# First bytes of the tiles of a decoder trunk, and the order of its mixer's steps

## The chip, the cores and the metric

The kernel runs on one core of one Trainium2 chip. The metric is the device time of one execution in microseconds; the time before is the median of three runs. The profile is that of one execution, taken by the hardware profiler. All times inside it count from the start of its span.

## The reference, cut to what matters

The input is one sequence of 512 tokens with 1024 channels, in float32. There are two layers; each is a mixer and then an MLP, and both of these parts are normed before (`rms_norm`) and after, and added to the residual stream.

```python
def trunk(x):
    for layer in (0, 1):
        h = rms_norm(x, mix_pre_g[layer])
        if layer == 0:                      # averages over 2, 4, 8, 16 tokens, less the token itself,
            m = pool_mixer(h, pool_w, pool_scale)   # then a 256x256 map for each of 4 channel groups
        else:                               # stick-breaking attention, 16 heads of 64; its k and v
            q = h @ w_q                     # were made from x after layer 0
            m = stick_breaking_attention(q, k, v) @ w_o
        x = x + rms_norm(m, mix_post_g[layer])
        h = rms_norm(x, mlp_pre_g[layer])
        u = h @ w_up[layer]                 # 1024 -> 4096
        x = x + rms_norm(square(relu(u)) @ w_down[layer], mlp_post_g[layer])   # 4096 -> 1024
        if layer == 0:
            k, v = split(rms_norm(x, kv_norm_g) @ w_kv)
    return x
```

## The kernel before, in words

**Three products for one.** Nearly all matrix products are made of a high and a low part of each operand, both in a 4-byte type that TensorE takes in one pass (fp32r). `split` makes them: ScalarE casts the high part, VectorE subtracts it from the source for the low part. A product is then three matmuls: high by high, high by low, low by high. Each matmul loads its 128x128 stationary operand (a LDWEIGHTS, PEld in the profile) and streams a moving operand of up to 512 columns (2048 bytes of each partition) past it. The load for the next matmul runs while the one before it streams.

**The stages.** The mixer of layer 0 comes first (some 49 us). Its work is cut into about 180 small steps, and `MIX_ORDER` lists them by hand: the letter is a step, the digits are a tile of 128 tokens and a half of the channels (tile 4 is the border between tiles, the tile `edge`). Every engine executes its own steps in this order. `q` squares a row of x on ScalarE and sums it, `r` takes the power of the sum on GpSimd, `b` scales the band matrix on VectorE, `P` averages on TensorE, `c` copies the result into `yt` on ScalarE, `L` scales the 256x256 maps on VectorE, `M` multiplies by them on TensorE, `s` and `g` square and weight what comes out, `T` transposes the normed tile, `H` and `X` split the transpose into `xnh` and `xnl`, and `U` is the first half (256 tokens) of one of the first four up products of the MLP.

Then come the MLP of layer 0 (to 366 us), its norms, the attention (to about 636 us) and the MLP of layer 1 (to the end).

**The MLP.** The up product of one block of 128 hidden channels (`up_block`) is 8x3 matmuls: a block of the weight is stationary (tiles `w` and `wx`, two halves high and low), the transposed tokens `xnh` and `xnl` move.

```python
for k in range(KC):     # L606 to L609; wh and wl are the two halves of a tile w
    nc.tensor.matmul(pu[:, cols], wh[:, k, :], xnh[:, k, cols], start=k == 0, stop=False)
    nc.tensor.matmul(pu[:, cols], wh[:, k, :], xnl[:, k, cols], start=False, stop=False)
    nc.tensor.matmul(pu[:, cols], wl[:, k, :], xnh[:, k, cols], start=False, stop=k == KC - 1)
```

Of the 32 blocks of hidden channels 28 go down through Strassen's seven products (class `Seven`, in five groups of two or three pairs of blocks), and the last four through a plain product (`contract`, lines L267 to L269, tiles `sq` and `dn`). In a Strassen product the tokens' operand `a` is stationary (made in `left`) and the weights' operand `w` moves (made in `right`). Both have two buffers, which take turns. A product is 12 matmuls in the first group and 18 in the others (L497); between two products one or two up blocks of the next group run.

**The attention.** The k and q projections are also `up_block`s (one pair of heads each), the v projection is a `contract`-like loop with 256 columns, and the output projection is `contract` again, with `ohl` (the heads' outputs) stationary and `w` moving; for the last two of its eight channel blocks the weights lie in the attention's own tiles `v`, `h` and `l`.

**First bytes.** The tiles are laid out one behind another in each partition, in the order in which they are first asked for, so that the size of a small tile sets the first byte of all that come behind it. The small tiles `gc` (96 bytes) and `stat` (32 bytes each) lie ahead of the large ones. In the program as built the first bytes are, for the tiles that TensorE reads most:

| tile | read as | before | modulo 256 | after | modulo 256 | after, modulo 512 |
|---|---|---|---|---|---|---|
| `xnh`, `xnl` | moving (up), stationary (v) | 17536, 33920 | 128, 128 | 17664, 34048 | 0, 0 | 256, 256 |
| `w`, `wx` | stationary (up), moving (output) | 96000 and every 8192 | 0 | 96256 and every 8192 | 0 | 0 |
| `a` of the products | stationary | 168704, 174848 | 0, 0 | 168960, 175360 | 0, 0 | 0, 256 |
| `w` of the products | moving | 187136, 199424 | 0, 0 | 187904, 201216 | 0, 0 | 0, 0 |
| `ohl` | stationary | 208192 and every 4096 | 64 | 208640 and every 4096 | 0 | 256 |
| `v`, `h`, `l` of the attention | moving (output), stationary | 145728, 170304, 175424 | 64 | 146176, 170752, 175872 | 0 | 256 |
| `sq`, `dn` | stationary, moving | all | 0 | all | 0 | 0 |

The pieces of a tile that a single matmul reads begin whole multiples of 512 bytes behind its first byte.

Of the kernel before, what the change touches and what calls it, by code (L numbers as in the profile page):

```python
# [42 lines left out]
    (w[0], [int(c) for c in w[1:]])  # L43
    for w in """z8 S0 q0 C0 S1 r0 b0 z1 P00 L00 L02 C1 c00 P01 L03 q4 L01 L13 r4 L10 L11 c01 L12 M00 M01 b4 q1 r1 b1 s00
    q2 s01 g00 e0 r2 P40 c40 g01 E0 b2 A0 P10 q3 c10 P11 r3 w0 P20 b3 v0 c11 M10 N00 P30 N01 h0 M11 T00 P31
    l0 s10 h1 c30 g10 s11 l1 c20 e1 g11 H00 E1 A1 X00 c31 h2 T01 M30 M31 w1 v1 l2 s30 N10 s31 M20 H01 N11 T10
    g31 P21 X01 H10 T11 c21 H11 M21 s21 X10 X11 e3 s20 g30 E3 U0 A3 w3 g21 e2 g20 h3 E2 A2 w2 v3 U1 N30 N31
    v2 l3 N21 T30 H30 U2 T21 T31 H31 N20 H21 T20 X30 X31 H20 X21 X20 U3""".split()
]
# [11 lines left out]

EDGE, REST, BORDER = 30, 114, 46

R_SCALE, R_MIX_POST0, R_MLP_PRE0, R_MLP_POST0, R_MIX_POST1, R_MLP_PRE1, R_MLP_POST1 = range(7)
# [5 lines left out]
def trunk(ctx, tc, x, consts, gcol, grow, pw, wup, wdn, wq, wk, wv, wo, out):  # L70
# [12 lines left out]
    def name(s):  # L83
        uid[0] += 1
        return f"{s}{uid[0]}"
# [6 lines left out]
    ident = keep.tile([P, P], F32, tag="ident", name="ident")  # L92
    gc = keep.tile([P, 3 * KC], F32, tag="gc", name="gc")
    for n in NS:
# [310 lines left out]
    class Seven:  # L405
# [17 lines left out]

        def __init__(self, l, first, n, mp):
            self.l, self.first, self.n, self.mp = l, first, n, mp
            self.banks, self.written, self.operands = {}, None, {}

        def load(self, second):
# [15 lines left out]
        def left(self, i):  # L444

            n, key = self.n, self.PRODUCTS[i][1]
            lo, hi = slice(0, S // 2), slice(S // 2, S)
            r11, r21, r12, r22 = (self.r[:, k, :n, h] for k in range(2) for h in (lo, hi))
            if i == 0:
                self.s1 = self.mp.tile([P, MOST, S // 2], F32, tag="s1", name=name("s1"))  # L450
            s1 = self.s1[:, :n]
            sub = lambda out, x, y, op=ALU.subtract: nc.gpsimd.tensor_tensor(out=out, in0=x, in1=y, op=op)  # L452
            if key == "s3":
                sub(s1, r21, r22, ALU.add)
                sub(r21, r11, r21)
                sub(r11, s1, r11)
            elif key == "r22":
                sub(r11, r12, r11)
            src = {"r11": r11, "s3": r21, "s2": r11, "r22": r22, "s1": s1, "r12": r12, "s4": r11}[key]
            a = self.mp.tile([P, 2, MOST, S // 2], F32R, tag="a", bufs=2, name=name("a"))  # L460
            split(src, a[:, 0, :n], a[:, 1, :n])
            return a

        def right(self, i):
# [15 lines left out]
            src = {"w11": w11, "t3": e, "t2": e, "t4": e, "t1": w12, "w21": w21, "w22": w22}[key]  # L480
            w = self.mp.tile([P, 2, MOST, 512], F32R, tag="w", bufs=2, name=name("w"))
            split(src, w[:, 0, :n], w[:, 1, :n])
# [25 lines left out]
    def mlp(l, mp, update):  # L508
# [4 lines left out]
        plain = 2 * sum(GROUPS)  # L513
        groups = [Seven(l, firsts[g], n, mp) for g, n in enumerate(GROUPS)]

# [96 lines left out]
    with tc.tile_pool(name="mix0", bufs=1, reuse_waits="tile") as mp:  # L612
# [9 lines left out]
        for w in windows.values():  # L622
            nc.vector.memset(w[:, D:], (EPS * D) ** 0.5)

# [59 lines left out]
        def squares(t):  # L684
            sts[t] = keep.tile([P, 8], F32, tag=f"stat{t}", bufs=4, name=name("stat"))
            mean_square(t, 0)
# [126 lines left out]
    with tc.tile_pool(name="att", bufs=1, reuse_waits="tile") as ap:  # L813
# [260 lines left out]
```

## Time and profile before

| | |
|---|---|
| time, median of 3 runs | 972.52 us (972.29 to 977.75) |
| the profiled execution: its time, its span | 971.85 us, 970.0 us |
| mean granted TensorE clock | 0.997 |
| TensorE busy | 951.6 us, 4761 matmuls |
| VectorE, ScalarE, GpSimd busy | 709.8, 568.7, 144.2 us |
| DMA | 157 MB, 45% of the 16 engines' span |

A row of the groups names the line, the engine, the operation, the tiles (out<-in), the shapes and the count; behind the first bar stand the busy time of the group and the mean nanoseconds of one. Matmuls overlap: one of 512 columns is busy for some 390 ns, but the next one starts some 230 ns after it. So what a matmul costs is the distance between two starts, and that is read from the starts in the timeline, or from the lengths in the chain of work that ended last, where a row "x18" is as long as it took until the next row began.

### The profile page before, as it was taken

The page shows a single profiled execution, that of the slowest core. Times are in us where ns is not written, and L with a number is a line of the kernel's source. Part 1 is how long each engine was busy: PE and PEld are TensorE (multiplying, and loading weights), DVE is VectorE, ACT ScalarE, POOL GpSimd, SP SyncE. Part 2 cuts the span into 40 slices and gives each one's busy share as a digit, 9 for nine tenths or more (in the row PEclk, how much of TensorE's full clock was granted, in tenths as well). Part 3 has the DMA queues.
Part 4 walks back from the last instruction along what each step waited for, and adds up shares of the span by engine and source line. Part 5 has one row for each costly group of instructions (what it writes and reads, how often), then busy time and mean ns, then how long its engine had stood idle before and what let it go on. Part 6 is the DMA issues. An engine that isn't in the chain of part 4 may idle for free.

```text
span 970.0 us, 12402 instructions
## 1 busy us (share of the span) xinstructions
PE 951.6 (98%) x4761; PEld 801.0 (83%) x4761; DVE 709.8 (73%) x736; ACT 568.7 (59%) x974; POOL 144.2 (15%) x108
## 2 busy tenths in 40 slices
PE   8999999999999999999999999989999999999997
PEld 6998888888888889888788887888888888888885
DVE  4856797988969966576477787855596876857856
ACT  6657889788865636455655563555544444443632
POOL 2120310502204014000000000301130300403103
PEclk9999999999999999999999999999999999999999
DMA  7544879697696840521624243332503233132012
GB/s 260 187 140 147 309 265 372 228 330 278 232 333 262 304 151 2 217 88 44 244 104 174 88 153 109 131 111 85 191 26 134 105 123 117 44 130 109 29 37 87
DMA packets 43683, 157.03 MB, mean 162 GB/s; under 512 B 4494, under 2 KB 4878, under 8 KB 43625
## 3 DMA queue, kind: packets, MB, share of 16 engines
q1 hardware_dynamic: 43625, 156.25, 45.0%
q8 instruction: 37, 0.61, 0.2%
q14 instruction: 21, 0.17, 0.1%
HBM read 122.68 MB, written 33.55 MB: 161 GB/s over the span
## 4 chain that ended last, share of the span: by engine, by line
PE 92%; DVE 3%; ACT 2%; issue 1%; DMA 1%; SPq 0%; POOL 0%; DVEq 0%; POOLq 0%; ACTq 0%
PE ps L497 28%; PE ps L609 15%; PE ps L607 15%; PE ps L608 15%; PE ps L268 4%; PE ps L269 4%; PE ps L267 4%; PE ps L957 2%; PE ps L947 1%; PE ps L731 1%; DVE e L929 1%; PE ps L915 1%; PE ps L916 1%; DMA edge<-in_x 1%; PE ps L708 1%
## 5 line engine op out<-in xcount | busy, mean ns | idle before, releaser
L497 PE MATMUL ps<-w,a 128*128 128x512 f32 x1176 | 278.8, 390 | 0.0
L608 PE MATMUL ps<-xnl,w 128*128 128x512 f32 (+1 forms) x712 | 265.0, 372 | 0.1
L609 PE MATMUL ps<-xnh,w 128*128 128x512 f32 (+1 forms) x712 | 265.1, 373 | 0.0
L607 PE MATMUL ps<-xnh,w 128*128 128x512 f32 (+1 forms) x712 | 265.0, 373 | 0.0
L497 PEld LDWEIGHTS ps<-w,a 128*128 128x128 f32 x1176 | 220.9, 188 | 47.4
L608 PEld LDWEIGHTS ps<-xnl,w 128*128 128x128 f32 x712 | 134.3, 189 | 25.2 <-DVE xnl L247 0.3
L609 PEld LDWEIGHTS ps<-xnh,w 128*128 128x128 f32 x712 | 134.1, 188 | 25.4
L607 PEld LDWEIGHTS ps<-xnh,w 128*128 128x128 f32 x712 | 134.0, 189 | 24.4
L134 DVE TENSOR_TENSOR w<-raw,w 128x1024 fp32r<-128x1024 f32 x62 | 82.2, 1328 | 62.7 <-ACT w L132 62.7
L132 ACT CAST w<-raw 128x1024 fp32r<-128x1024 f32 x62 | 65.0, 1049 | 87.8 <-PE ps L609 83.4
L506 DVE TENSOR_TENSOR y<-ps,y 128x512 f32<-128x512 f32 x124 | 83.4, 684 | 39.7 <-PE ps L497 39.7
L246 ACT CAST a<-r 128x768 fp32r<-128x768 f32 (+1 forms) x60 | 47.5, 792 | 70.5 <-PE ps L497 46.8
L452 POOL TENSOR_TENSOR s<-r 128x768 f32<-128x768 f32 (+1 forms) x10 | 20.5, 2048 | 382.0 <-ACT r L530 382.0
L247 DVE TENSOR_TENSOR a<-r,a 128x768 fp32r<-128x768 f32 (+1 forms) x60 | 60.1, 1004 | 18.5 <-ACT a L246 18.4
L246 ACT CAST w<-e 128x1536 fp32r<-128x1536 f32 (+1 forms) x30 | 42.0, 1398 | 44.5 <-DVE e L471 33.2
L292 POOL TENSOR_TENSOR y<-y,grow 128x512 f32<-128x512 f32 x12 | 18.7, 1556 | 316.4 <-ACT xn L250 316.4
L452 POOL TENSOR_TENSOR r<-r 128x768 f32<-128x768 f32 (+1 forms) x20 | 52.2, 2608 | 59.3 <-DVE a L247 58.5
L247 DVE TENSOR_TENSOR w<-e,w 128x1536 fp32r<-128x1536 f32 (+1 forms) x30 | 55.9, 1862 | 3.1 <-ACT w L246 2.7
L929 DVE TENSOR_TENSOR_SCAN e<-u,begin 128x1280 f32<-128x1280 f32 x16 | 45.1, 2822 | 13.3 <-ACT u L923 13.0
L143 ACT ACTIVATE apart<-apart,gc 128x128 f32<-128x128 f32 (+1 forms) x132 | 43.0, 405 | 0.0
L250 ACT ACTIVATE xn<-y 128x512 f32<-128x512 f32 (+1 forms) x25 | 15.4, 615 | 41.8 <-DVE y L359 41.8
L247 DVE TENSOR_TENSOR w<-xn,w 128x1536 fp32r<-128x1536 f32 (+1 forms) x20 | 33.0, 1651 | 6.4 <-ACT w L246 6.4
(137 smaller groups left out, 1486.5 us busy)
## 6 DMA issues: line engine op xcount, KB each, us to landing
raw<-in_wup SPq DMA_DIRECT2D x62, 512.0 KB, 4.1
w<-kept SPq DMA_DIRECT2D x58, 512.0 KB, 4.1
kept<-wx SPq DMA_DIRECT2D x30, 512.0 KB, 4.3
w<-in_wdn SPq DMA_DIRECT2D x8, 1536.0 KB, 6.7
kept<-apart SPq DMA_DIRECT2D x24, 512.0 KB, 3.6
xn<-in_wdn SPq DMA_DIRECT2D x8, 1536.0 KB, 8.0
raw<-in_wdn SPq DMA_DIRECT2D x8, 512.0 KB, 3.7
apart<-in_wk SPq DMA_DIRECT2D x7, 512.0 KB, 6.5
```

What stands on the lines that cost most here:

```text
L132: nc.scalar.copy(hi, raw)
L134: nc.vector.tensor_tensor(out=lo, in0=raw, in1=hi.bitcast(F32), op=ALU.subtract)
L143: nc.scalar.mul(c, c, gc[:, lo + k : lo + k + 1])
L246: latest["act"] = nc.scalar.copy(hi, src)
L247: latest["dve"] = nc.vector.tensor_tensor(out=lo, in0=src, in1=hi.bitcast(F32), op=ALU.subtract)
L452: sub = lambda out, x, y, op=ALU.subtract: nc.gpsimd.tensor_tensor(out=out, in0=x, in1=y, op=op)
L497: nc.tensor.matmul(bank, a[:, x, q, TS[t]], w[:, z, q], start=start and q == 0 and k == 0, stop=q == self.n - 1 and k == 2, skip_group_che ...
L506: nc.vector.tensor_tensor(out=part, in0=bank, in1=part, op=ALU.add)
L607: nc.tensor.matmul(pu[:, cols], wh[:, k, :], xnh[:, k, cols], start=k == 0, stop=False)
L608: nc.tensor.matmul(pu[:, cols], wh[:, k, :], xnl[:, k, cols], start=False, stop=False)
L609: nc.tensor.matmul(pu[:, cols], wl[:, k, :], xnh[:, k, cols], start=False, stop=k == KC - 1)
L929: nc.vector.tensor_tensor_scan(out=e[:, ::-1], data0=u[:, 1:][:, ::-1], data1=begin[:, ::-1], initial=0.0, op0=ALU.mult, op1=ALU.max,)
```

## The change

Three things, none of which changes what is computed. Small tiles are padded (`gc` by 128 bytes, the `stat` of the border by 32 in each of its four buffers, `u1` by 220), which moves the first bytes of the tiles behind them as in the table. The tiles `a` and `w` of the Strassen products become flat with 256 and 1024 spare bytes, and in layer 1 (only there: `self.l`) product number 7g+i, of the 35, puts its `a` at byte 64 times (7g+i) modulo 5 of the tile, and its `w` at entry (7g+i) modulo 7 of 0, 64, 128, 192, 256, 512 and 1024 bytes, so that each of the 35 pairs comes once. And `MIX_ORDER` is another list of the same steps.

```diff
+A_PLACES, W_PLACES = (0, 16, 32, 48, 64), (0, 16, 32, 48, 64, 128, 256)
...
-    gc = keep.tile([P, 3 * KC], F32, tag="gc", name="gc")
+    gc = keep.tile([P, 3 * KC + 32], F32, tag="gc", name="gc")[:, : 3 * KC]
...
+        def place(self, i, places):
+            return places[(7 * self.g + i) % len(places)] if self.l else 0
...
-            a = self.mp.tile([P, 2, MOST, S // 2], F32R, tag="a", bufs=2, name=name("a"))
+            a = self.mp.tile([P, MOST * S + 64], F32R, tag="a", bufs=2, name=name("a"))
+            at = self.place(i, A_PLACES)
+            a = a[:, at : at + MOST * S].rearrange("p (x n c) -> p x n c", x=2, n=MOST)
...
-            w = self.mp.tile([P, 2, MOST, 512], F32R, tag="w", bufs=2, name=name("w"))
+            w = self.mp.tile([P, MOST * D + 256], F32R, tag="w", bufs=2, name=name("w"))
+            at = self.place(i, W_PLACES)
+            w = w[:, at : at + MOST * D].rearrange("p (x n c) -> p x n c", x=2, n=MOST)
...
-            sts[t] = keep.tile([P, 8], F32, tag=f"stat{t}", bufs=4, name=name("stat"))
+            sts[t] = keep.tile([P, 16 if t == T else 8], F32, tag=f"stat{t}", bufs=4, name=name("stat"))
...
-        us = [ap.tile([P, NSEG + 1], F32, tag=f"u{a}", name=f"u{a}") for a in range(2)]
+        us = [ap.tile([P, NSEG + 1 + 55 * a], F32, tag=f"u{a}", name=f"u{a}")[:, : NSEG + 1] for a in range(2)]
...
-    for w in """z8 S0 q0 C0 S1 r0 b0 z1 P00 L00 L02 C1 c00 P01 L03 q4 L01 L13 r4 L10 L11 c01 L12 M00 M01 b4 q1 r1 b1 s00
+    for w in """z8 q0 S0 r0 C0 b0 S1 z1 P00 L01 C1 L02 L00 P01 L03 L12 c00 c01 M00 q4 L10 r4 L11 s00 L13 b4 q1 r1 M01 s01
```

What the new list does to the engines shows at two places. The first is ScalarE at the start of the mixer: `junk,stat<-edge` is step `q4`, `yt<-ps` are the copies `c00` and `c01`, `junk,stat<-ps` are the squares of a mixed tile. Before:

```order
L723 COPY yt<-ps_143 128x4x128
L679 ACTIVATE junk,stat_158<-edge 90x1025
L723 COPY yt<-ps_152 128x4x128
L679 ACTIVATE junk,stat_179<-x_71 128x1025
L250 ACTIVATE junk,stat_134<-ps_167 128x512
```

And now:

```order
L731 COPY yt<-ps_143 128x4x128
L731 COPY yt<-ps_152 128x4x128
L687 ACTIVATE junk,stat_166<-edge 90x1025
L251 ACTIVATE junk,stat_132<-ps_161 128x512
L687 ACTIVATE junk,stat_175<-x_71 128x1025
```

The second copy stood behind the step that reads `edge`; now it stands ahead of it. The second place is VectorE behind the scaling of the maps: `band<-bands` are the steps `b` (90 partitions is `b4`), `stat<-stat` is step `e0`, which adds two sums of squares. Before:

```order
L667 SCALAR_TENSOR_TENSOR pw_100<-pw_100,gc,scale 128x256 x4
L698 TENSOR_SCALAR band_177<-bands,stat_158 90x184
L698 TENSOR_SCALAR band_182<-bands,stat_179 128x456
L739 TENSOR_TENSOR m_188<-ps_167,grow_112 128x512
L743 TENSOR_SCALAR stat_134<-stat_134 128x1
```

And now:

```order
L675 SCALAR_TENSOR_TENSOR pw_100<-pw_100,gc,scale 128x256 x4
L706 TENSOR_SCALAR band_173<-bands,stat_166 90x184
L751 TENSOR_SCALAR stat_132<-stat_132 128x1
L706 TENSOR_SCALAR band_194<-bands,stat_175 128x456
L747 TENSOR_TENSOR m_216<-ps_161,grow_112 128x512
```

The sum `e0` now stands ahead of `b1`, the band for the first whole tile. Behind the mixer the order of instructions is the same on every engine, but for a few neighbours that change places.

More of the change, by code (lines that the diff above doesn't have):

```diff
@@ L43 @@
     (w[0], [int(c) for c in w[1:]])
-    for w in """z8 S0 q0 C0 S1 r0 b0 z1 P00 L00 L02 C1 c00 P01 L03 q4 L01 L13 r4 L10 L11 c01 L12 M00 M01 b4 q1 r1 b1 s00
[L45 to L48, printed above, removed]
+    for w in """z8 q0 S0 r0 C0 b0 S1 z1 P00 L01 C1 L02 L00 P01 L03 L12 c00 c01 M00 q4 L10 r4 L11 s00 L13 b4 q1 r1 M01 s01
+    e0 P40 b1 P11 P10 q2 c40 r2 c11 E0 q3 g00 b2 g01 r3 c10 P21 A0 b3 M11 w0 M10 s11 c21 v0 P31 N00 g11 s10
+    T00 P30 h0 M21 e1 c31 g10 E1 c30 N01 A1 P20 H00 T01 w1 X00 h1 v1 l0 s21 N11 M30 T11 c20 N10 T10 H01 M20
+    l1 H11 X11 H10 X10 s30 M31 X01 h2 s20 h3 g21 l2 s31 g20 e2 g30 E2 e3 E3 U0 A2 w2 g31 U1 A3 v2 U2 l3 N20
+    w3 T20 H20 v3 N31 T31 N30 N21 T30 H31 X20 X31 T21 H30 X30 U3 H21 X21""".split()
 ]
@@ L422, in trunk, with __init__ @@
         )
-        def __init__(self, l, first, n, mp):
-            self.l, self.first, self.n, self.mp = l, first, n, mp
+        def __init__(self, l, g, first, n, mp):
+            self.l, self.g, self.first, self.n, self.mp = l, g, first, n, mp
             self.banks, self.written, self.operands = {}, None, {}
+        def place(self, i, places):
+            return places[(7 * self.g + i) % len(places)] if self.l else 0
         def load(self, second):
@@ L513, in mlp @@
         plain = 2 * sum(GROUPS)
-        groups = [Seven(l, firsts[g], n, mp) for g, n in enumerate(GROUPS)]
+        groups = [Seven(l, g, firsts[g], n, mp) for g, n in enumerate(GROUPS)]
         steps = [n for n in range(1, 34)] if l == 0 else []
@@ L622, in trunk @@
         for w in windows.values():
-            nc.vector.memset(w[:, D:], (EPS * D) ** 0.5)
+            nc.vector.memset(w[:, D : D + 2], (EPS * D) ** 0.5)
         BANDS = (P, REST, BORDER)
```

## The prediction

> **What bounds the kernel now.** I read the totals and the chain of work that ended last first, then the busy times of the three long stages.
>
> ```profile
> PE 951.6 (98%) x4761; PEld 801.0 (83%) x4761; DVE 709.8 (73%) x736; ACT 568.7 (59%) x974; POOL 144.2 (15%) x108
> PE 92%; DVE 3%; ACT 2%; issue 1%; DMA 1%; SPq 0%; POOL 0%; DVEq 0%; POOLq 0%; ACTq 0%
> 49.00:366.00 317.00, 317.00 (x1425) 260.71 (x1424) 258.45 (x232) 231.64 (x384) 57.58 (x26) 1.00 0.71 256
> 385.00:636.00 251.00, 244.35 (x1436) 215.06 (x1435) 175.71 (x210) 136.15 (x302) 10.57 (x12) 0.99 0.37 133
> 636.00:955.00 319.00, 319.00 (x1443) 262.94 (x1443) 223.16 (x201) 152.91 (x187) 52.66 (x24) 1.00 0.27 94
> ```
>
> TensorE bounds it: 92% of the chain, and in the two MLPs (first and third stretch) it is busy for the whole stretch, at the full granted clock (1.00). So what changes the distance between two matmuls there changes the time one for one, while the next engine, VectorE with 258.45 of 317 us, has room.
>
> The second look is at that distance. The groups, with shapes kept apart, show that matmuls of one shape are not equal:
>
> ```profile
> L497 PE MATMUL ps<-w,a 128*128 128x512 f32 x1176 | 278.8, 390 | 0.0
> L607 PE MATMUL ps<-xnh,w 128*128 128x512 f32 x568 | 224.4, 395 | 0.0
> L267 PE MATMUL ps<-dn,sq 128*128 128x512 f32 x60 | 23.5, 392 | 0.0
> L268 PE MATMUL ps<-w,ohl 128*128 128x512 f32 x56 | 22.4, 399 | 2.2 <-DVE w L134 2.2
> ```
>
> All stream 512 columns. The Strassen products (L497) and the plain down product (`dn`, `sq`) last 390 to 392 ns, the up products (L607, and L608 and L609 with it) and the output projection (`ohl`) 395 and more. The chain of the second MLP and the timeline of one up block give the distances:
>
> ```profile
> 742.10 4.10 PE ps L497 x18
> 761.48 8.18 PE ps L497 x36
> ...
> 798.55 0.39 PE L607 MATMUL ps<-xnh,w 128*128 128x512 f32 x1
> ...
> 804.14 2.22 PE L497 MATMUL ps<-w,a 128*128 128x512 f32 x9
> ```
>
> One product is 18 matmuls in 4.10 us, two in a row 8.18, so the second takes 4.08: 226.7 ns each. (The 0.02 us that the first takes more are the turn from the up block before it.) The up block's 24 matmuls take from 798.55 to 804.14, 5.59 us: 232.9 each. The difference is 6.2 ns.
>
> What differs is the first bytes. I call the distance of a pair the first byte of the moving operand less that of the stationary operand which is loaded meanwhile, modulo 256. From the table of first bytes: products 0, `dn` with `sq` 0, up products 128 (`xnh` at 128, `w` at 0), output projection 192 (`w` at 0, `ohl` at 64). The longer ones are those whose distance is not 0. That it is the distance, and not whether each operand begins at a multiple of 256, shows where the output projection takes its weights from `h` and `l`, which begin at 64 as `ohl` does, and then again from `w`:
>
> ```profile
> 601.40 0.39 PE L269 MATMUL ps<-h,ohl 128*128 128x512 f32 x1
> ...
> 602.30 0.39 PE L267 MATMUL ps<-w,ohl 128*128 128x512 f32 x1
> ...
> 603.71 0.39 PE L267 MATMUL ps<-w,ohl 128*128 128x512 f32 x1
> ```
>
> The last four of the run with `h` and `l` take 0.90 us, 225 ns each; the next six, with `w`, 1.41 us, 235 each. Same line, same stationary tile, nothing waited for.
>
> At 256 columns there is no such difference:
>
> ```profile
> 36.07 0.28 PE L608 MATMUL ps<-xnl,w 128*128 128x256 f32 x1
> ...
> 41.23 0.29 PE L609 MATMUL ps<-xnh,w 128*128 128x256 f32 x1
> ...
> 959.95 0.28 PE L268 MATMUL ps<-dn,sq 128*128 128x256 f32 x1
> ...
> 962.59 0.28 PE L269 MATMUL ps<-dn,sq 128*128 128x256 f32 x1
> ```
>
> 43 steps in 5.16 us at distance 128, 22 steps in 2.64 us at distance 0: 120 ns both. Half up blocks and the v projection, all of 256 columns, so count nothing.
>
> **The change part by part.** *Padding, up products of the MLPs.* `xnh`, `xnl` and `w` all go to multiples of 256: distance 0. Each MLP has 28 whole up blocks (the first four are cut in halves), 672 matmuls, 1344 in both, all on a full TensorE: 1344 x 6.2 ns = **-8.3 us**. One thing in it is unknown: modulo 512 the new distance is 256, which no pair of this trace has (all the short ones are 0 modulo 512, and tiles that differ by 512 were among them). Its cost is bounded by the two rows above, 226.7 and 232.9, or may lie outside them. I take 226.7: the same products had 0 and 512 alike, so the period is 512 or a part of it; 64 and 128 are excluded as periods, since 192 and 128 are long; and the sizes speak for the smaller one. By the rows at both widths, 256 more columns cost 226.7 - 120.0 = 106.7 ns, so the 512 columns alone are 213.4 and the rest 13.3 ns; of a long pair the rest is 19.5. That is two units of some 6.6 ns against three. A load takes 512 bytes of each partition, which is two turns of a period of 256: two meetings, and three where they don't begin in step. With a period of 512 it would be one against one and a half. This is a fit, not a proof: I hold 256 the likelier, about three to one.
>
> *Padding, attention.* 1704 up matmuls (3 x 568) less 1344 are 360 in the k and q projections; of the output projection 148 go from distance 192 to 0 (modulo 512 to 256). 508 x 6.2 = 3.2 us. Here the chain is not TensorE's throughout:
>
> ```profile
> 447.73 0.60 ACT u L923
> 466.67 0.50 PE ps L267
> 568.83 0.62 ACT ah L246 x2
> 583.56 0.50 PE ps L268
> 614.55 0.72 ACT xn L250 x2
> 634.00 1.94 PE ps L324 x8
> ```
>
> Between the first and second, third and fourth, fifth and sixth of these rows it runs over ScalarE and VectorE: 19 + 15 + 19 = 53 of 251 us, in which a faster TensorE only waits longer. I count the other 79%: **-2.5 us** (bounds 0 and -3.2).
>
> *Products of layer 0.* Distance 0 stays 0 modulo 256. The turns of 0.02 us from an up block to a product go, some 30 of them: **-0.5 us**. Modulo 512 the two buffers of `a` now differ, so that every second product has 256: the same unknown.
>
> *Products of layer 1.* From the 35 pairs, 11 have distance 0 modulo 256, and of the 588 matmuls 422 have another: at 6.2 ns **+2.6 us**. A distance of 64 (146 matmuls) is not in the trace; bounds -0.9 and, at twice the price, +0.9 against that; I take the price of 128 and 192, which agree.
>
> *The mixer's list.* The rows of its start:
>
> ```profile
> 4.75 7.44 DMA edge<-in_x
> 12.37 1.06 ACT L679 ACTIVATE junk<-edge 90x1025 f32<-90x1025 f32 x1 [3.56 <-DMA edge<-in_x]
> 13.42 0.56 ACT L723 COPY yt<-ps 128x512 f32<-128x512 f32 x1
> 13.89 1.06 ACT L679 ACTIVATE junk<-x 128x1025 f32<-128x1025 f32 x1
> 15.07 0.60 ACT L250 ACTIVATE junk<-ps 128x512 f32<-128x512 f32 x1
> 14.18 0.31 DVE L698 TENSOR_SCALAR band<-bands,stat 90x184 f32<-90x184 f32 x1 [2.24 <-POOL stat L690]
> 14.04 1.99 PE L731 MATMUL ps<-pw,yt 128*128 128x256 f32 x8 [2.62 <-ACT yt L723]
> 15.87 1.88 PE L708 MATMUL ps<-band,edge 90*128 90x46 f32 x16
> 17.57 2.91 PE L708 MATMUL ps<-band,x 128*128 128x114 f32 x24
> 35.41 0.47 PE L607 MATMUL ps<-xnh,w 128*128 128x256 f32 x1
> ```
>
> `c01` (13.42) stood behind `q4`, which waited for the DMA of `edge`; M01 on TensorE waited 2.62 us for it, and P40 (15.87) for M01. Ahead of `q4` the copy is done by 9, and M01 well before 14. P40 then waits for its band alone (14.18 + 0.31), and begins at 14.55: 1.3 us sooner. Next, P11 needs `b1`, which now stands behind `e0`, and that waits for ScalarE's `s01`: q4 to 13.5, s00 0.7, q1 1.2, s01 0.7, so 16.1, and `b1` is done by 16.7. P40 takes 1.70 and ends at 16.25: 0.45 us of the gain is lost. From there to the end of U3 TensorE has the same matmuls as before and was busy without a gap worth naming, so if no other step is late the stage ends **-0.9 us** sooner. What is late next would be VectorE's chain from `A2` over `A3` to `N20`, ahead of the transposes that stand between U2 and U3; they have the 8.6 us of U0 to U2 to hide under. Bounds -1.3 (no wait at all) and +1 (a wait of 2 us there).
>
> Nothing else moves. **Sum:** -8.3 - 2.5 - 0.5 + 2.6 - 0.9 = -9.6. Against the profiled execution's own 971.85 us (span 970.0) that is 962.3; the median of the three runs is 0.7 higher and gives 962.9. I say 962.5.
>
> **The rivals.** *First bytes count modulo 512.* For it: every short pair of the trace is 0 there. Then the up and output products stay as they are, every second product of layer 0 becomes longer (270 matmuls x 6.2 = +1.7), of layer 1 only 95 matmuls stay short (493 x 6.2 = +3.1, and +0 for the padding). With the mixer's -0.9: +3.9, 976.
>
> *First bytes don't count at all,* and up blocks are longer for another reason, such as reading one stationary block twice in a row. Against it speak the rows with `h` and `l`. Then the list alone is left, -0.9: 971. The Trainium skill's page "SBUF — State Buffer", section "Who interferes with whom", has this rule: it gives TensorE two read ports of its own, one for the moving operand and one for the load, and says that "PE and ACT never wait on anyone". By that rule all rows of 512 columns would be equal; the trace, with 390 and 395 ns, disagrees.
>
> *Slower: half a period is the worst place.* If the period is 512 and the distance of 256 costs one more step of 6.2 ns, to 239, then the 1344 up matmuls and 148 + 360 of the attention pay it (+10.9 at 79% of the latter), 270 products of layer 0 pay two steps (+3.3), layer 1 some +3.4: with the list +16.7, 988.5. It decides from about half a step, 3 ns, on: +9.7 is 1%. No row shows a run of matmuls that long.
>
> *Another engine takes over.* VectorE's share in the first MLP would rise from 258 of 317 to 258 of 313 us; if buffers then come late, half of the -8.3 goes: 966.5. *Better pairs.* If an unseen distance were faster than 226.7 by a step, the padding's 256 above all: 950 to 958.
>
> **How the numbers follow.** Chances: forecast 0.62, modulo 512 0.18, no effect 0.04, half period worst 0.06, another engine 0.06, better pairs 0.04. A measurement of this kernel tells a change from none by about 1%, 9.7 us, which is 962.8: my forecast sits on that line, so half of its chance is on either side, a little more on the near side. Faster by over 1%: 0.33 + 0.04; within 1%: 0.29 + 0.18 + 0.04 + 0.06; slower: 0.06. The forecast's own range, from all of the attention's gain, a short distance of 64 and the mixer's best down to the lowest bounds of these, is 959.5 to 967. To leave out no more than 2 in 10 it has to reach to the modulo-512 case, so 958 to 977.
>
> **What would show it.** In the profile after: L607's successor at 390 ns instead of 395, and its blocks 5.44 us long instead of 5.59; the product rows of layer 0 at 4.08; in layer 1, products of 4.08 and of 4.20 side by side, by their pair; P40 at 14.5 and the first up block 0.9 us sooner. Up rows that stay at 395 with layer 0's products alternating between 390 and 395 would mean modulo 512; rows over 400, the slower case.

## The result, and the profile after

The changed kernel takes 966.43 us (median of 6 runs, 963.89 to 967.43) against 972.45 for the kernel before in the same rounds: a ratio of 0.9919, with a 95% interval of 0.9894 to 0.9944. That is 6 us, where 10 were forecast. The profiled execution took 966.99 us (span 965.2), 4.86 less than the one of before.

The chain of work that ended last, of the changed kernel, and then its two MLPs by engine (behind the length of the stretch stand the busy times of TensorE, its weight loads, VectorE, ScalarE and GpSimd):

```profile
PE 78%; DVE 9%; DMA 4%; issue 4%; ACT 3%; SPq 0%; POOL 0%; POOLq 0%; DVEq 0%; ACTq 0%
```

```profile
49.00:366.00 317.00, 314.99 (x1432) 261.89 (x1432) 259.21 (x232) 231.96 (x387) 62.42 (x26) 1.00 0.72 255
636.00:955.00 319.00, 319.00 (x1443) 263.92 (x1442) 224.21 (x203) 152.50 (x189) 56.52 (x26) 1.00 0.27 94
```

TensorE had 92% of the chain, now 78%; VectorE went from 3 to 9%, DMA from 1 to 4%. In the first MLP TensorE is no longer busy for the whole stretch: 314.99 of 317 us. In the second it still is. The groups, with shapes kept apart, name the row that waits:

```profile
L505 PE MATMUL ps<-w,a 128*128 128x512 f32 x1176 | 280.5, 391 | 2.0 <-DVE a L248 1.4 <-DVE w L248 0.5
L615 PE MATMUL ps<-xnh,w 128*128 128x512 f32 x568 | 221.4, 390 | 0.0
```

The up products (L615 to L617) are at 390 ns, where they had 395. The Strassen products had no idle time before; now they wait 2.0 us, for the operands that VectorE makes.

From the starts of the matmuls I worked out how long each stage takes, in microseconds (the first MLP from the end of U3 to the end of its last Strassen product, the attention from there to the first product of the second MLP, the second MLP from its first product to the end of its last). The waits, here and in all that follows, are counted from the starts too: by how much two starts lie further apart than 226.7 ns, where that is over 0.1 us. That takes in the slower matmul behind each pause, so it is more than the idle time of 2.0 us above.

| | mixer, first matmul to U3 | first MLP | its waits | attention | second MLP | sum of changes |
|---|---|---|---|---|---|---|
| before | 47.49 | 305.84 | 0 | 301.44 | 288.80 | |
| after | 47.51 | 304.13 | 2.82 | 300.01 | 287.05 | |
| difference | +0.02 | -1.71 | | -1.43 | -1.75 | -4.87 |
| predicted | -0.9 | -4.65 | 0 | -2.5 | -1.55 | -9.6 |

The missing 4.7 us are 2.9 in the first MLP, 1.1 in the attention and 0.9 in the mixer, less 0.2 that the second MLP brought more.

### The profile page after: what moved, and what is told of

It is laid out like the page before. It is cut to its first block, busy times and chain, and to the rows that moved or that the text cites. A ratio compares the mean times of both kernels' runs of the same rounds, so it can differ in the third digit from the quotient of the medians.

```text
span 965.2 us, 12405 instructions
## 1 busy us (share of the span) xinstructions
PE 944.9 (98%) x4761; PEld 801.4 (83%) x4761; DVE 710.2 (74%) x736; ACT 567.4 (59%) x974; POOL 150.5 (16%) x108
## 4 chain that ended last, share of the span: by engine, by line
PE 78%; DVE 9%; DMA 4%; issue 4%; ACT 3%; SPq 0%; POOL 0%; POOLq 0%; DVEq 0%; ACTq 0%
PE ps L505 21%; PE ps L615 12%; PE ps L617 12%; PE ps L616 12%; PE ps L269 4%; PE ps L270 4%; PE ps L268 4%; DMA xn<-in_wdn 2%; PE ps L965 2%; PE ps L955 2%; DVE w L135 1%; DVE w L248 1%; DVE e L477 1%; PE ps L739 1%; DVE y L514 1%
## 5 line engine op out<-in xcount | busy, mean ns | idle before, releaser
L615 PE MATMUL ps<-xnh,w 128*128 128x512 f32 (+1 forms) x712 | 262.3, 370 | 0.0
L617 PE MATMUL ps<-xnh,w 128*128 128x512 f32 (+1 forms) x712 | 262.1, 369 | 0.0
L617 PEld LDWEIGHTS ps<-xnh,w 128*128 128x128 f32 x712 | 134.6, 189 | 22.4
L615 PEld LDWEIGHTS ps<-xnh,w 128*128 128x128 f32 x712 | 134.4, 189 | 22.1
L456 POOL TENSOR_TENSOR r<-r 128x768 f32<-128x768 f32 (+1 forms) x20 | 58.3, 2916 | 66.2 <-DVE a L248 65.4
```

## The experiments

The version without places (all the rest of the change) is the base of most of them, since its two MLPs differ in nothing of the first bytes.

### The list alone

The kernel before, with the new `MIX_ORDER` and no other edit.

```diff
-    for w in """z8 S0 q0 C0 S1 r0 b0 z1 P00 L00 L02 C1 c00 P01 L03 q4 L01 L13 r4 L10 L11 c01 L12 M00 M01 b4 q1 r1 b1 s00
+    for w in """z8 q0 S0 r0 C0 b0 S1 z1 P00 L01 C1 L02 L00 P01 L03 L12 c00 c01 M00 q4 L10 r4 L11 s00 L13 b4 q1 r1 M01 s01
...
```

> The kernel before with the new list of the mixer's steps alone. Theory A (the distances carry the change, the list next to nothing, and what is missing of the gain is TensorE waiting for VectorE in layer 0): within 0.5 us of the kernel before, 972.0 to 973.0, and the first up block's end within 0.3 us. Theory B (the list moves the start of the weights' DMAs and costs what is missing): slower by 2 to 4 us, 974.5 to 976.5, with new waits of TensorE between 180 and 260 us. The prediction on record said -0.9: 971.5.

Measured: 970.83 us (10 runs) against 972.19, a ratio of 0.9993 with an interval of 0.9978 to 1.0008. From the first matmul to U3 the profiled execution took 45.75 us, 1.74 less than before; the other stages agree with before to 0.3 us. By time the list can't be told from no change, and theory B's loss of 2 to 4 us isn't there. By stage it gained in this execution, more than the 0.3 us that theory A allowed; the table of all runs at the end of this section shows how much that varies.

### The padding alone

The old list, the new padding, no places.

```diff
-A_PLACES, W_PLACES = (0, 16, 32, 48, 64), (0, 16, 32, 48, 64, 128, 256)
+A_PLACES, W_PLACES = (0,), (0,)
...
     (MIX_ORDER as before)
```

> The padding alone: the old list, and all products of layer 1 at distance 0. Theory A: the full gain of the up and output products less the waits in layer 0, and none of layer 1's cost, some 2.2 us under the changed kernel: 963.5 to 965. Theory B: also without the list's cost, 960.5 to 962.

Measured: 963.70 us, a ratio of 0.9915 (0.9896 to 0.9933). The first MLP 302.61 us with 1.30 us of waits, the attention 301.40, the second MLP 284.24. So the padding is the gain, and the second MLP gets it whole: -4.56 us.

### The change without places

```diff
-A_PLACES, W_PLACES = (0, 16, 32, 48, 64), (0, 16, 32, 48, 64, 128, 256)
+A_PLACES, W_PLACES = (0,), (0,)
```

> The changed kernel with every product of layer 1 at distance 0 (padding and new list). From the changed kernel's trace, the 422 matmuls at other distances cost 146 x 2.2 + 139 x 6.1 + 137 x 6.7 ns = 2.1 us: both theories expect 2.1 us less than the changed kernel, 964.0 to 964.6, all of it between 650 and 942 us. If the places cost nothing, 966.4.

Measured: 962.02 us (961.73 to 966.89), a ratio of 0.9919 (0.9892 to 0.9945). The first MLP 302.97 with 1.63 us of waits, the attention 299.77, the second MLP 284.24: the places cost the second MLP 287.05 - 284.24 = 2.81 us, more than the 2.1 expected.

### Steps of 16 bytes

`a` stays at 0, and the products of layer 1 put `w` at 0, 16, ... 240 bytes in turn, which gives every distance that is a multiple of 16.

```diff
-A_PLACES, W_PLACES = (0, 16, 32, 48, 64), (0, 16, 32, 48, 64, 128, 256)
+A_PLACES, W_PLACES = (0,), tuple(range(0, 64, 4))
```

> The changed kernel, but in layer 1 all the stationary operands stand at 0 and product number k has its moving operand 16 x (k modulo 16) bytes behind: distances in steps of 16 bytes over the whole period of 256. If the distance works in steps of 64 bytes (a bank of that width), 0 to 48 give 226.7 ns, 64 to 112 give 228.9, then 233. If it is the meeting of two streams, the time rises smoothly or in steps of 16, and some distance near 0 may be below 226.7. The total is not the question: 965 to 968.

Measured: 966.46 us, the second MLP 288.15. The mean distance between two starts in nanoseconds, from the starts in the trace, in each product from the matmul on from which it is steady (to about half a nanosecond, since the starts repeat unevenly):

| first bytes' distance | 0 | 16 | 32 | 48 | 64 | 80 | 96 | 112 |
|---|---|---|---|---|---|---|---|---|
| ns | 226.6 | 231.5 | 233.5 | 233.4 | 228.9 | 231.4 | 233.8 | 230.6 |

| distance | 128 | 144 | 160 | 176 | 192 | 208 | 224 | 240 |
|---|---|---|---|---|---|---|---|---|
| ns | 232.9 | 233.3 | 234.0 | 231.3 | 233.3 | 234.8 | 233.3 | 233.3 |

The changed kernel gives the same at its four distances: 226.7 at 0, 228.9 at 64, 232.8 at 128, 233.3 at 192. Pairs with both operands at 128, or both at 192, settle at 226.7 too. The one product with both at 64 is at 230.6 over its twelve matmuls and comes down to 227 only with the last two. Its uneven starts (228, 230, 233, 236, 224 ns apart, and so on) return one by one in the up block behind the product with both at 192, and that block settles at 226.7 after ten matmuls: it is a turn, and this product is hardly longer than the turn. So it is the distance, as the prediction took from `h` and `l`, which with `ohl` are both at 64 and settle at 226.8 in the trace of before. No distance is better than 0. Nothing goes in steps of 64 bytes or in two or three prices. In the chain of the changed kernel the products of layer 1 show it row by row (18 matmuls each, at distances 128, 64, 0 and 192):

```profile
747.85 4.19 PE ps L505 x18
...
765.68 0.23 PE ps L615
...
771.12 4.14 PE ps L505 x18
...
809.51 4.08 PE ps L505 x18
...
852.13 4.20 PE ps L505 x18
```

From the row at 765.68 to the one at 771.12 runs one up block: 24 matmuls in 5.44 us, 226.7 each, where it was 5.59.

### Less work on VectorE

From here on the question is the waits of the first MLP. The subtraction that makes the low part of the weights ahead of time (L197, `apart` and `wx`) is done for 8 columns instead of 1024.

```diff
-                nc.vector.tensor_tensor(out=raw, in0=raw, in1=hi.bitcast(F32), op=ALU.subtract)
+                nc.vector.tensor_tensor(
+                    out=raw[:, :8], in0=raw[:, :8], in1=hi[:, :8].bitcast(F32), op=ALU.subtract
+                )
```

> On the padded kernel with all products at distance 0: VectorE's subtractions for the weights that are made ahead in layer 0 (31 of 1.2 us) shortened to 8 of 1024 columns, which leaves out the low parts of those weights. The kernel without this had TensorE wait 1.6 us in layer 0 (2.8 in the changed kernel, 0 in the kernel before). Theory V (VectorE has too much to do there): waits under 0.3 us. Theory G (its instructions are stretched by GpSimd's): waits shrink in part, as fewer instructions are there to be stretched. Theory L (the down weights' load of 1.5 MB comes late): waits stay over 1.3.

Measured: 959.87 us; the first MLP 301.23 us with no wait, the attention 300.04, the second MLP 284.24. That speaks against theory L; it fits V, and G too, since fewer instructions are left to be stretched.

### Short sums on GpSimd

Every instruction stays where it is; three of the four sums that GpSimd makes for each group of layer 0 cover 8 of 256 columns.

```diff
-            sub = lambda out, x, y, op=ALU.subtract: nc.gpsimd.tensor_tensor(out=out, in0=x, in1=y, op=op)
+            cut = (lambda z: z) if self.l else (lambda z: z[:, :, :8])
+            sub = lambda out, x, y, op=ALU.subtract: nc.gpsimd.tensor_tensor(
+                out=cut(out), in0=cut(x), in1=cut(y), op=op
+            )
...
-                sub(s1, r21, r22, ALU.add)
+                nc.gpsimd.tensor_tensor(out=s1, in0=r21, in1=r22, op=ALU.add)
```

> The same kernel, but three of GpSimd's four subtractions for each group of layer 0 take 8 of 256 columns, which leaves out most of those Strassen sums; no instruction changes its place. Theory G: VectorE's stretched instructions (2.9 instead of 1.2 us) go, and TensorE's waits in layer 0 with them, under 0.4 us. Theories V and L: waits stay over 1.3 us, since VectorE has as much to do and the load is as late.

Measured: 959.05 us; the first MLP 301.23 us, no wait. The same gain as with less work on VectorE, without an instruction less there. The same stretch of the first MLP by engine (the third pair is VectorE, the fifth GpSimd), first for the version without places:

```profile
49.00:366.00 317.00, 316.16 (x1435) 262.64 (x1434) 261.24 (x237) 233.86 (x391) 59.97 (x28) 1.00 0.72 255
```

and for the short sums:

```profile
49.00:366.00 317.00, 317.00 (x1444) 264.24 (x1444) 248.93 (x240) 237.00 (x398) 43.84 (x29) 1.00 0.72 253
```

With the short sums VectorE is busy 248.93 us, where the version without places had 261.24 with the same instructions. What GpSimd does, then, makes VectorE's work longer. The timeline of the changed kernel shows where it comes from:

```profile
230.01 1.76 DVE L477 TENSOR_TENSOR e<-xn,w 128x1536 f32<-128x1536 f32 x1 [2.58 <-DMA xn<-in_wdn]
230.81 8.32 PE L505 MATMUL ps<-w,a 128*128 128x512 f32 x36
231.69 1.75 DVE L248 TENSOR_TENSOR w<-w,w 128x1536 fp32r<-128x1536 f32 x1
233.30 1.84 POOL L456 TENSOR_TENSOR s<-r 128x768 f32<-128x768 f32 x1 [42.41 <-ACT r L538]
233.36 2.87 DVE L197 TENSOR_TENSOR apart<-apart,wx 128x1024 f32<-128x1024 f32 x1
235.23 2.72 POOL L456 TENSOR_TENSOR r<-r 128x768 f32<-128x768 f32 x1
236.15 3.41 DVE L477 TENSOR_TENSOR w<-w 128x1536 f32<-128x1536 f32 x1
238.03 3.24 POOL L456 TENSOR_TENSOR r<-s,r 128x768 f32<-128x768 f32 x1
239.48 2.87 DVE L135 TENSOR_TENSOR w<-raw,w 128x1024 fp32r<-128x1024 f32 x1
243.47 1.74 DVE L248 TENSOR_TENSOR w<-e,w 128x1536 fp32r<-128x1536 f32 x1
245.27 0.96 PE L505 MATMUL ps<-w,a 128*128 128x512 f32 x3 [0.47 <-DVE w L248]
245.74 1.21 DVE L197 TENSOR_TENSOR apart<-apart,wx 128x1024 f32<-128x1024 f32 x1
249.14 1.81 DVE L248 TENSOR_TENSOR a<-r,a 128x768 fp32r<-128x768 f32 x2
250.13 2.12 PE L505 MATMUL ps<-w,a 128*128 128x512 f32 x8 [1.39 <-DVE a L248]
...
251.03 7.26 POOL L456 TENSOR_TENSOR r<-r 128x768 f32<-128x768 f32 x1 [9.76 <-DVE a L248]
252.54 1.21 DVE L197 TENSOR_TENSOR apart<-apart,wx 128x1024 f32<-128x1024 f32 x1
```

While GpSimd's three sums run (233.30 to 241.27), three instructions of VectorE take 2.87, 3.41 and 2.87 us; alone, 128x1024 takes 1.21 (245.74) and 128x1536 takes 1.75 (231.69). That is 4.98 us more. The next operands, `w` at 243.47 and `a` at 249.14, come too late, and TensorE waits 0.47 and 1.39. (The view of the row at 250.13 ends at 252 us, so it counts 8 matmuls; 14 run there.)

The rows read as if the two engines took turns by whole instructions. VectorE's first long one ends at 236.23, 1.1 us behind the end of GpSimd's first sum (235.14), about what it takes alone. Nor is it always VectorE that is held up: GpSimd's next sum, at 251.03, takes 7.26 us, and VectorE's subtraction beside it (252.54) only 1.21. No run was made to test this order.

The Trainium skill's page "SBUF — State Buffer", section "Who interferes with whom", says that an instruction of VectorE with two inputs in SBUF contends with one of GpSimd that reads SBUF, since its second input comes through the shared read interface. The trace agrees: 2.87 us beside 1.21.

### A shorter load

VectorE starts that stretch late, because it waits 2.58 us for a DMA (230.01). The second load of the down weights of layer 0's later groups is cut from 1.5 to 0.5 MB; the scheduler moves a few instructions for it.

```diff
-            nc.sync.dma_start(w[:, :n], src[1 if second else 0])
+            m = 1 if second and self.l == 0 and self.first else n
+            nc.sync.dma_start(w[:, :m], src[1 if second else 0][:, :m])
```

> The same kernel, but the second load of down weights of each group of layer 0 brings one of three blocks, 0.5 instead of 1.5 MB (the other two keep what was there, which leaves out their weights). Theory L: the load lands 4 us sooner, VectorE doesn't wait for it, TensorE's waits in layer 0 under 0.4 us. Theories G and V: over 1.3 us.

Measured: 963.17 us; the first MLP 303.55 us with 2.30 us of waits, 2.19 of them in one place:

```profile
116.18 3.40 DVE L248 TENSOR_TENSOR w<-w,w 128x1536 fp32r<-128x1536 f32 x1
119.63 2.57 PE L506 MATMUL ps<-w,a 128*128 128x512 f32 x10 [2.03 <-DVE w L248]
```

With a third of the load the waits are as long in sum, and again behind an instruction that took 3.40 us beside a sum of GpSimd (of 3.23 us, from 114.73 on). But they have moved: the three places that waited in the version without places (185, 247 and 307 us) are free, and VectorE's instructions stand in another order, so this run alone doesn't clear the load. The sums on VectorE, below, do: there VectorE waits 5.0 us for this DMA in the first MLP, and TensorE hardly waits.

### The changed kernel once more

No edit.

> The changed kernel once more, timed beside the kernel before on this chip, to set it against the kernels of the first set: 963.9 to 967.4 as before. In the trace: waits of TensorE in layer 0 of 1.3 to 3.6 us, at about 186, 244 and 248 us if they belong to the program, elsewhere if they come from the DMAs' chance order; the products of layer 1 at 226.7, 228.9, 233 and 233.4 ns by distance as in the first profile.

Measured: 965.97 us (5 runs), a ratio of 0.9937 (0.9916 to 0.9957). The first MLP 302.39 us with 1.06 us of waits (under the 1.3 expected; at 185, 247 and 306 us), where the first profile had 304.13 with 2.82 (at 187, 245 and 250); the second MLP 287.05 again, to the hundredth. So what the first MLP loses differs from execution to execution, and what the distances cost doesn't.

### The up products back at 128

The version without places, with only `xnh` and `xnl` back at 128 modulo 256; all later tiles stay where they were.

```diff
-    gc = keep.tile([P, 3 * KC + 32], F32, tag="gc", name="gc")[:, : 3 * KC]
+    gc = keep.tile([P, 3 * KC], F32, tag="gc", name="gc")
...
-    xnl = keep.tile([P, KC, S], F32R, tag="xnl", name="xnl")
+    xnl = keep.tile([P, KC * S + 32], F32R, tag="xnl", name="xnl")[:, : KC * S].rearrange("p (k s) -> p k s", k=KC)
```

> The version without places, and of the first bytes only those of xnh and xnl back at 128 modulo 256 (gc without its padding, the 128 bytes behind xnl instead, so that all later tiles stay where they were). The instructions and their order are those of the version without places. Theory D (the distance sets the pitch, and layer 0 waits only because the quicker up blocks catch up with VectorE): up matmuls of 512 columns 233 ns, products 226.7; the first MLP 305.8 us with less than 0.5 us of waits, the second 288.8. Rival N (the waits of layer 0 come with the new order of steps and the new first bytes as such, whatever TensorE's speed): the first MLP 306.5 to 308, with 1 to 3 us of waits. Rival S (what counts is that each operand starts at a multiple of 256, not the distance): the same as D here for the up matmuls. Time by D 969 to 972, by N 970 to 975.

Measured: 968.88 us, one run, just under what D expected. The first MLP 305.92 us and no wait, the second 288.79; up matmuls 233.0 ns. Theory D holds: give the up products their 6.2 ns back, and the waits go with them, though VectorE's instructions are as long as ever:

```profile
234.48 2.88 DVE L135 TENSOR_TENSOR w<-raw,w 128x1024 fp32r<-128x1024 f32 x1
```

So VectorE was always that slow there: over the whole stretch its instructions of 1024 and 1536 columns take some 20 us longer than they do alone, in the kernel before, in the changed kernel and here. A slower TensorE didn't notice. Between D and S this run doesn't tell; the pairs with both operands at 128 or 192 do, for D.

### The sums on VectorE

If GpSimd's sums delay VectorE by more than they are long there, VectorE should make them itself, in layer 0.

```diff
-            sub = lambda out, x, y, op=ALU.subtract: nc.gpsimd.tensor_tensor(out=out, in0=x, in1=y, op=op)
+            on = nc.gpsimd if self.l else nc.vector
+            sub = lambda out, x, y, op=ALU.subtract: on.tensor_tensor(out=out, in0=x, in1=y, op=op)
```

> The version without places, with the sums of the tokens' Strassen operands in layer 0 on VectorE instead of GpSimd (in layer 1 they stay on GpSimd); the scheduler moves some 20 groups of instructions by a few places for it. Theory G (VectorE is late in layer 0 because its instructions with two inputs are stretched while GpSimd subtracts): no VectorE row of 128x1024 in the first MLP takes longer than 1.3 us, the waits there are under 0.5 us, the first MLP takes 301.2 us and the whole 959 to 962. Rival V (VectorE is late because it has too much work, and some 25 us more of it makes it later still): the first MLP 303 to 310 us with waits of 2 to 8 us, the whole 962 to 970.

> The version without places once more, on the same chip as the sums on VectorE, for the comparison and for what differs between two executions. Layer 1 284.2 us as before; the first MLP 301.2 to 304, by how many waits fall into this execution; time 960 to 964.

Measured: 961.28 us (960.48 to 962.19), a ratio of 0.9880 (0.9864 to 0.9897); the version without places, beside it on the same chip, 962.05 us and 0.9899 (0.9877 to 0.9922). The first MLP takes 301.67 us with 0.41 us of waits, against 302.61 with 1.32. The groups of VectorE in the first MLP, with the sums there (the number behind the bar is the mean of one):

```profile
L197 DVE TENSOR_TENSOR apart<-apart,wx 128x1024 f32<-128x1024 f32 x24 | 29.2, 1218 | 0.6 <-ACT wx L196 0.6
L478 DVE TENSOR_TENSOR e<-xn,w 128x1536 f32<-128x1536 f32 x4 | 7.0, 1755 | 5.0 <-DMA xn<-in_wdn 5.0
```

the stretch by engine:

```profile
49.00:366.00 317.00, 316.86 (x1445) 264.04 (x1444) 256.04 (x256) 233.03 (x391) 7.07 (x8) 1.00 0.72 256
```

and with the sums on GpSimd, in the version without places run beside it:

```profile
L197 DVE TENSOR_TENSOR apart<-apart,wx 128x1024 f32<-128x1024 f32 x24 | 32.5, 1354 | 0.3 <-ACT wx L196 0.3
L477 DVE TENSOR_TENSOR e<-xn,w 128x1536 f32<-128x1536 f32 x4 | 8.7, 2170 | 4.7 <-DMA xn<-in_wdn 4.7
```

and its stretch by engine:

```profile
49.00:366.00 317.00, 316.22 (x1438) 262.95 (x1437) 261.09 (x237) 234.31 (x393) 59.56 (x28) 1.00 0.72 253
```

Theory G holds and V falls: VectorE does 19 instructions more in this stretch and is busy 5 us less. L falls too: VectorE waits 5.0 us for the load here, and TensorE 0.41. All of it together beats the kernel before by 12 us in the same rounds, and the changed kernel by its ratio to the kernel before (0.9864 to 0.9897 here, 0.9916 to 0.9957 when the changed kernel ran once more); against the version without places the intervals overlap, so that the 0.8 us between the two is shown by the stage, not by the time.

### All runs by stage

| run | mixer | first MLP | its waits | attention | second MLP |
|---|---|---|---|---|---|
| list alone | 45.75 | 305.88 | 0 | 301.67 | 288.82 |
| padding alone | 47.25 | 302.61 | 1.30 | 301.40 | 284.24 |
| without places | 46.47 | 302.97 | 1.63 | 299.77 | 284.24 |
| steps of 16 bytes | 45.05 | 304.93 | 3.63 | 300.02 | 288.15 |
| less work on VectorE | 46.38 | 301.23 | 0 | 300.04 | 284.24 |
| short sums on GpSimd | 45.36 | 301.23 | 0 | 299.93 | 284.24 |
| shorter load | 47.01 | 303.55 | 2.30 | 300.09 | 284.24 |
| changed again | 46.50 | 302.39 | 1.06 | 301.49 | 287.05 |
| up products at 128 | 44.80 | 305.92 | 0 | 301.10 | 288.79 |
| sums on VectorE | 48.07 | 301.67 | 0.41 | 299.95 | 284.24 |
| without places again | 45.97 | 302.61 | 1.32 | 301.32 | 284.24 |

## Why the prediction was right or wrong

**What bounds the kernel, and the period: right.** The distance modulo 256 sets what a matmul of 512 columns costs. The up pairs, at 256 modulo 512, are at 226.7 ns in the first MLP, so the modulo-512 case is refuted, and with it half a period as the worst place. That first bytes count for nothing is refuted by the second MLP's -4.56 us. The prediction's fit behind it ("two units of some 6.6 ns against three") is wrong all the same: with 228.9 at a distance of 64 and 230.6 to 234.8 between, there are no two prices. The choice of 256 came out right on an argument that did not hold.

**The up products of the MLPs: the step that failed.** 1344 x 6.2 = 8.3 us was counted in full, "all on a full TensorE". In the second MLP that holds. In the first, TensorE was full before, and no longer is once it is quicker: 2.82 us of waits in the profiled execution, 1.06 in the other one. The rows that should have warned were in the trace of before:

```profile
230.28 1.76 DVE L471 TENSOR_TENSOR e<-xn,w 128x1536 f32<-128x1536 f32 x1 [0.57 <-DMA xn<-in_wdn]
233.23 8.34 PE L497 MATMUL ps<-w,a 128*128 128x512 f32 x36
235.72 2.51 POOL L452 TENSOR_TENSOR s<-r 128x768 f32<-128x768 f32 x1 [44.73 <-ACT r L530]
236.43 2.88 DVE L134 TENSOR_TENSOR w<-raw,w 128x1024 fp32r<-128x1024 f32 x1
240.43 2.21 DVE L247 TENSOR_TENSOR w<-e,w 128x1536 fp32r<-128x1536 f32 x1
243.15 2.27 DVE L196 TENSOR_TENSOR apart<-apart,wx 128x1024 f32<-128x1024 f32 x1
247.62 1.81 DVE L247 TENSOR_TENSOR a<-r,a 128x768 fp32r<-128x768 f32 x2
250.48 3.36 PE L497 MATMUL ps<-w,a 128*128 128x512 f32 x14
```

The row at 247.62 is two instructions, each for another `a`. The first is done at 248.56, and the product that takes it goes on at 250.48: VectorE was 1.9 us ahead there. In the profile after, the products ahead of it begin 2.42 us sooner (230.81 for 233.23), and VectorE's instruction behind the DMA only 0.27 sooner (230.01 for 230.28). A slack of 1.9 us doesn't cover these 2.15, and VectorE then falls back further: the same `a` is done at 250.08, 1.5 us later than before. GpSimd's sums begin 2.42 us sooner with the products (233.30 for 235.72) and meet more of VectorE's long instructions: VectorE loses 4.98 us to them here, where it lost 3.2 (the rows at 236.43, 240.43 and 243.15). The prediction read VectorE's busy share, 258 of 317 us, which says nothing of the tightest place.

**The rival "another engine takes over" came true, and had 0.06.** Its place (VectorE in the first MLP) and its mechanism (operands come late) fit what was measured. That its time, 966.5, fits too is luck: it gave away half of 8.3 us there, where the waits were 2.82, and the attention and the mixer lost the rest. It deserved several times that chance. The cause of the lateness, VectorE's instructions stretched by GpSimd's sums, was in no part of the prediction.

**The products of layer 0** kept their price, and the turns went: without waits the first MLP takes 301.23, which is -4.61 for the -4.65 of both terms together.

**The pairs of layer 1: right in size, by errors that cancel.** +2.6 predicted, +2.81 measured. Distance 64 costs 2.2 ns and not 6.2. Within the products the matmuls cost 2.1 us more than at distance 0. But the up blocks between the products are longer too: 227.5 ns on average over 619 matmuls, 226.7 in the version without places, another 0.5 us (the rest is in the turns). The places are a plain loss.

**The attention: -2.5 predicted, -1.43 measured, -1.67 without places.** Part of the miss is in the price: the up matmuls gain 5.0 ns (232.7 to 227.7), the 192 of the output projection 4.3 on average, since 24 of them already had their weights from `h` and `l` and gain 3.0. That makes 381 x 5.0 + 192 x 4.3 = 2.7 us on the engine instead of 3.2. The rest is in the share. When TensorE goes on behind its last long wait (at 630.57, before at 634.00), 1.75 us have arrived, 65% and not 79%. And at this place every run has a stretch of 3.41 us in which the granted clock is 0.50. First the stretch in the kernel before, then in the changed one:

```profile
633.42:636.83 3.41, 2.83 (x14) 2.86 (x15) 2.02 (x4) 1.44 (x3) 0.00 (x0) 0.50 0.00 0
630.97:634.38 3.41, 3.41 (x18) 3.18 (x16) 1.96 (x4) 2.12 (x3) 0.00 (x0) 0.50 0.30 43
```

Before, it begins while TensorE still waits, so that 2.83 us of work fall into it; in the changed kernel it is all 3.41. The 0.58 us more at half the clock cost 0.29, about what is lost between 1.75 and 1.43. A larger effect sits further ahead. The output projection waits 2 us for VectorE's `w` in every run. In the version without places and in the changed kernel's first profile nothing follows; with the padding alone, this:

```profile
578.72 0.50 PE L269 MATMUL ps<-w,ohl 128*128 128x512 f32 x1 [1.97 <-DVE w L135]
579.06 0.40 PE L270 MATMUL ps<-w,ohl 128*128 128x512 f32 x1
579.29 0.57 PE L269 MATMUL ps<-w,ohl 128*128 128x512 f32 x1
...
580.51 0.63 PE L270 MATMUL ps<-w,ohl 128*128 128x512 f32 x1
580.94 0.63 PE L269 MATMUL ps<-w,ohl 128*128 128x512 f32 x1
```

The stretch around it by engine, with the granted clock third from the end:

```profile
570.00:596.00 26.00, 24.03 (x130) 20.57 (x128) 21.66 (x27) 9.23 (x20) 0.00 (x0) 0.93 0.41 141
```

The matmuls go from 0.23 us apart to 0.43, and the granted clock of these 26 us is 0.93; in the kernel before it was 1.00. Again it is one stretch of 3.41 us at 0.50, and it costs about 1.5 us by the starts. The attention takes 299.77 us in one execution of the version without places and 301.32, with such a stretch, in the other. The changed kernel shows both cases as well (300.01 and 301.49). So a single execution can lose nearly all of the attention's gain to something that the same kernel doesn't show in another.

**The mixer's list: right by its chain, lost in the DMA and the transposes.** The start of the changed kernel:

```profile
11.25 3.69 PE L739 MATMUL ps<-pw,yt 128*128 128x256 f32 x16 [1.59 <-DVE pw L675]
13.35 1.06 ACT L687 ACTIVATE junk<-edge 90x1025 f32<-90x1025 f32 x1 [3.07 <-DMA edge<-in_x]
15.53 1.98 PE L716 MATMUL ps<-band,edge 90*128 90x46 f32 x16 [0.59 <-DVE band L706]
35.15 0.47 PE L615 MATMUL ps<-xnh,w 128*128 128x256 f32 x1
43.33 2.08 DVE L764 SCALAR_TENSOR_TENSOR xn<-x,stat,spare 128x512 f32<-128x512 f32 x3 [0.44 <-POOL stat L698]
43.96 2.16 PE L773 MATMUL ps<-ident,xn 128*128 128x128 f32 x16
```

M01 no longer holds P40 up: it is through by 14.94 (the row at 11.25). P40 waits for its band alone and begins 2.18 us behind `q4`, where it was 3.50: the 1.3 us of the prediction. `b1` behind `e0` costs P11 a wait of 0.28, for the 0.45 predicted. But the DMA of `edge` let `q4` start at 13.35 and not at 12.37, so that P40 is at 15.53, not at 14.5, and the first up block 0.26 us sooner, not 0.9; by the end of U3 (48.80 before, 48.82 after) that is gone too. It goes in the transposes between U2 and U3, where the prediction looked for what is late next: the last four of the sixteen at 43.96 begin at 45.46, right behind VectorE's third `xn` (the row at 43.33, done at 45.40), and the sixteen take 1.91 us until U3, 0.12 each, where the last twelve of before took 1.23, 0.10 each. The stage varies from 44.80 to 48.07 us over the runs with the same list, more than the term; three of these runs (46.50, 47.01 and 48.07) have a stretch of 3.41 us at half the granted clock in it. What landed when is not the list's, and by time its worth stays open.

**The number.** 962.5 was a sum of one term too large (the first MLP, by 2.9 us), one by 1.1 and one by 0.9. A time like it was reached in another kernel, and not by its sum: the version without places, at 962.02, has no cost of the places, and waits instead.

## What to carry to other kernels

Place the moving operand and the stationary operand that is loaded meanwhile so that their first bytes are equal modulo 256, and then leave them alone: on these matmuls of 512 columns it is nearly 3% (226.7 for 232.9 ns) for nothing. Before a gain is counted one for one on "the full engine", find the place where its suppliers have the least lead, in microseconds, and compare that with what the engine gains up to there; a busy share of 82% says nothing of it. Where VectorE is that supplier, look whether GpSimd runs beside it: here some 18 us of sums on VectorE were cheaper, by 0.9 us in the first MLP, than 52 us of the same sums on GpSimd.

## What the runs showed of the hardware that was not expected

- The price of a distance is not a step: 226.6 ns at 0, 228.9 at 64, 230.6 to 234.8 at the other multiples of 16 bytes up to 240, and at 0 it settles at the same whether both operands begin at 0, 128 or 192. Behind a change of the distance up to ten matmuls pass before the price is steady.
- It carries over: up matmuls at distance 0 take 227.5 ns on average where products at other distances stand between their blocks, and 226.7 where none do.
- A subtraction of VectorE with two inputs can take 2.87 instead of 1.21 us (128x1024), and 3.41 instead of 1.75 (128x1536), beside GpSimd's sums; elsewhere it is GpSimd's sum that takes 7.26. With the sums of layer 0 on VectorE no group of 128x1024 in the first MLP has a mean over 1.23 us.
- A wait of 2 us of TensorE in the output projection is followed in 3 of the 13 profiled executions, and not in others of the same kernel, by 3.41 us at half the granted clock, at a cost of about 1.5 us. Behind the wait of 3.3 us at the end of the attention such a stretch stands in all 13.
